# Output tiles of 16 tokens in two buffers, in place of 8 tokens in four

## The chip, the cores and the metric

The kernel runs on one core of a Trainium2 chip. The metric is the device time of a run in microseconds (us). Three runs of the kernel before gave a median of 240.93 us (240.78 to 241.42). The profile was taken of one further run of 240.54 us; its span, from the first to the last instruction of the program, is 238.8 us, and all times below that are positions in the trace count from the start of this span.

## The reference

```
batch, seq, hidden, n_experts = 16, 1024, 512, 8
k = 2
x:              (16, 1024, 512)  float32
expert_weights: (16, 1024, 2)    float32

x_expanded = x[:, :, np.newaxis, :].repeat(k, axis=2)
weights = expert_weights[..., np.newaxis]
return (x_expanded * weights).astype(np.float32)
```

Each of the 16,384 tokens is a row of 512 numbers. The output has two copies of each row, the first multiplied by the token's first weight and the second by its second weight. The expert indices are an input that is not used. 33.5 MB come in and 67.1 MB go out, and there is one multiplication for each number that goes out.

## The kernel before

The tokens are dealt to the 128 partitions in blocks: partition p holds tokens 128p to 128p + 127, so each partition has 128 tokens, which lie one after another in memory (`xr`, `outr` and `wr`, lines 27 to 33). A stretch of several tokens of one partition is therefore one contiguous row on both sides of a transfer.

All weights are loaded once, in one transfer of 128 KB issued by SyncE (line 45). The outer loop (line 47) runs over 8 input tiles of `TX` = 16 tokens for each partition. An input tile is 128 partitions x 8192 numbers, 4 MB, with rows of 32 KB, and is loaded on ScalarE's queue (line 49). The pool `x_pool` has two buffers, so a third load can be issued only when VectorE has read all of the first tile.

The inner loop (line 52) makes two output tiles of `TO` = 8 tokens from each input tile. For each token and each of its two weights, VectorE multiplies 512 numbers of the input tile by a weight, one weight for each partition, and writes them to the output tile (line 59). That is 16 multiplies for an output tile and 256 in all. Then SyncE issues the store of the output tile (line 67): 4 MB, with rows of 8 x 1024 numbers, 32 KB. The pool `o_pool` has four buffers, so the fifth output tile can be begun only when the first store has landed.

The framework puts in the waits: a multiply waits for its input tile's load and for the store that last used its output buffer; a store waits for the last multiply of its tile; a load waits for the last multiply that reads its buffer. Each engine keeps the order in which the program names its work. The order of the work is therefore set by the two queues and by the number of buffers, and by nothing else.

Of the kernel before, what the change touches and what calls it, by code (L numbers as in the profile page):

```python
# [1 line left out]

# [4 lines left out]


@with_exitstack
def kernel(  # L10
    ctx: ExitStack,
    tc: tile.TileContext,
    x: bass.AP,
    expert_indices: bass.AP,
    expert_weights: bass.AP,
    out: bass.AP,
):
    nc = tc.nc

    batch, seq, hidden = x.shape  # L20
    k = expert_weights.shape[-1]
    P = nc.NUM_PARTITIONS
    ntok = batch * seq
    assert ntok % P == 0
    A_TOTAL = ntok // P

    xr = x.rearrange("b s h -> (b s) h").rearrange("(p a) h -> p (a h)", a=A_TOTAL)
    outr = out.rearrange("b s k h -> (b s) (k h)").rearrange(
        "(p a) n -> p (a n)", a=A_TOTAL
    )  # L30
    wr = expert_weights.rearrange("b s k -> (b s) k").rearrange(
        "(p a) k -> p (a k)", a=A_TOTAL
    )
    f32 = mybir.dt.float32
    row = k * hidden

    TX = 16
    TO = 8

    w_pool = ctx.enter_context(tc.tile_pool(name="w_pool", bufs=1))  # L40
    x_pool = ctx.enter_context(tc.tile_pool(name="x_pool", bufs=2))
    o_pool = ctx.enter_context(tc.tile_pool(name="o_pool", bufs=4))

    w_tile = w_pool.tile([P, A_TOTAL * k], f32)
    nc.sync.dma_start(out=w_tile, in_=wr)

    for i in range(A_TOTAL // TX):
        x_tile = x_pool.tile([P, TX * hidden], f32)
        nc.scalar.dma_start(
            out=x_tile, in_=xr[:, i * TX * hidden : (i + 1) * TX * hidden]  # L50
        )
        for j in range(TX // TO):
            o_tile = o_pool.tile([P, TO * row], f32)
            for t in range(TO):
                at = (j * TO + t) * hidden
                for kk in range(k):
                    c = (i * TX + j * TO + t) * k + kk
                    o = t * row + kk * hidden
                    nc.vector.tensor_scalar(  # L59
                        out=o_tile[:, o : o + hidden],  # L60
                        in0=x_tile[:, at : at + hidden],
                        scalar1=w_tile[:, c : c + 1],
                        scalar2=None,
                        op0=mybir.AluOpType.mult,
                    )
            first = (i * TX + j * TO) * row
            nc.sync.dma_start(out=outr[:, first : first + TO * row], in_=o_tile)


# [1 line left out]
_INS = ['x', 'expert_indices', 'expert_weights']  # L71
_OUTS = [((16, 1024, 2, 512), 'float32')]


# [23 lines left out]
```

## Time and profile before

| what | value |
|---|---|
| time, median of 3 | 240.93 us |
| span of the profiled run | 238.8 us |
| VectorE busy | 102.5 us in 256 multiplies |
| read from and written to memory | 33.69 MB and 67.11 MB, 422 GB/s over the span |
| stores | 16 of 4096 KB, median 44.9 us from issue to landing |
| loads of the input | 8 of 4096 KB, median 23.9 us from issue to landing |
| load of the weights | 128 KB, 10.1 us from issue to landing |

On the page of the profile, the span is cut into 40 equal slices of about 6 us. Each digit of the row for DMA is the busy share of the core's 16 DMA engines in that slice in tenths, and the row of GB/s is what they moved. The queue that the page calls q1 is SyncE's (the stores and the weights), and q10 is ScalarE's (the loads of the input); for each queue the page gives the packets, the MB and the share of 16 engines' span that the packets took. In the list of waits, the three numbers are the total in us, how often, and the longest. In a list in order of time, a line has its start and length in us, the engine and line, the instruction with what it writes and reads, how many of them were joined, and in brackets the idle time before the first with what ended it. The name L59 is line 59 of the kernel.

### The profile page before, as it was taken

How to read it: one execution, taken by the hardware profiler on the slowest of the kernel's cores; microseconds unless marked ns; L12 is line 12 of the kernel's file. 1: busy time of each engine (PE TensorE's matmuls, PEld its weight loads, DVE VectorE, ACT ScalarE, POOL GpSimd, SP SyncE). 2: the span in 40 equal slices, each digit the busy share in tenths (PEclk: the TensorE clock that was granted, in tenths of full speed). 3: DMA queues.
4: the chain of work that ended last, by engine and by line, in shares of the span. 5: the costliest groups of instructions: out<-in, count | busy, mean ns of one | idle time of the engine just before them, and what ended most of it. 6: DMA issues, size and time to landing. Idle time of an engine off the chain costs nothing.

```text
span 238.8 us, 358 instructions
## 1 busy us (share of the span) xinstructions
DVE 102.5 (43%) x256; POOL 0.2 (0%) x4
## 2 busy tenths in 40 slices
DVE  0079994059701904682054910739008486400000
POOL 0000000000000000000000000000000000000000
DMA  7999999999999999999999999999999999999994
GB/s 277 447 439 417 434 380 417 439 439 439 423 423 428 439 423 412 439 439 439 439 439 434 434 439 439 412 435 428 428 423 434 434 439 439 439 439 434 434 439 214
DMA packets 3602, 100.81 MB, mean 422 GB/s; under 512 B 400, under 2 KB 528, under 8 KB 528
## 3 DMA queue, kind: packets, MB, share of 16 engines
q1 hardware_dynamic: 2448, 67.24, 65.4%
q10 hardware_dynamic: 1152, 33.55, 33.2%
q14 instruction: 2, 0.02, 0.0%
HBM read 33.69 MB, written 67.11 MB: 422 GB/s over the span
## 4 chain that ended last, share of the span: by engine, by line
DMA 62%; DVE 18%; another core or an unknown queue 5%; DVEq 0%; issue 0%
DMA out_dram<-o_tile 57%; DVE o_tile L59 18%; DMA x_tile<-in_x_dram 5%; DVEq L93 0%; DVEq L59 0%
## 5 line engine op out<-in xcount | busy, mean ns | idle before, releaser
L59 DVE TENSOR_SCALAR o_tile<-x_tile,w_tile 128x512 f32<-128x512 f32 x256 | 102.5, 480 | 103.3 <-DMA out_dram<-o_tile 74.1
L82 POOL MEMSET const-bfloat16-1.0<- 128x1 bf16 x1 | 0.1, 101 | 0.0
L82 POOL MEMSET const-uint8-127<- 128x1 uint8 x1 | 0.1, 101 | 0.0
L82 POOL MEMSET const-float32-0.0<- 128x1 f32 x1 | 0.1, 98 | 0.2 <-issue 0.2
L82 POOL MEMSET const-float32-1.0<- 128x1 f32 x1 | 0.1, 98 | 0.0
## 6 DMA issues: line engine op xcount, KB each, us to landing
out_dram<-o_tile SPq DMA_DIRECT2D x16, 4096.0 KB, 44.9
x_tile<-in_x_dram ACTq DMA_DIRECT2D x8, 4096.0 KB, 23.9
w_tile<-in_expert_weights_dram SPq DMA_DIRECT2D x1, 128.0 KB, 10.1
```

The costliest lines, as they stand in the source:

```text
L59: nc.vector.tensor_scalar(out=o_tile[:, o : o + hidden], in0=x_tile[:, at : at + hidden], scalar1=w_tile[:, c : c + 1], scalar2=None, op0= ...
L82: nc = _bacc.Bacc("TRN2", target_bir_lowering=False, num_devices=1)
```

## The change

Output tiles hold 16 tokens, as many as an input tile, so that each input tile gives one output tile of 8 MB, and a store has rows of 64 KB in place of 32 KB. There are two such output buffers in place of four of half the size, so the memory for them is the same: 128 KB of each partition. It is meant to store in fewer and longer pieces.

The code around it is written in a more general form: a list of groups, each with its tiles, each tile with the pieces in which it is loaded. Here there is one group of eight tiles with one piece each, so that `rows(x, 0, 128)` is the same split of the tokens as before, the weights are loaded in one transfer, and each input tile is loaded in one transfer of 16 tokens on ScalarE's queue, as before. A store is issued when a piece or an output tile ends, which is once for each input tile.

```diff
-    TO = 8
+    TO = 16
+    groups = [[[16], [16], [16], [16], [16], [16], [16], [16]]]
...
-    o_pool = ctx.enter_context(tc.tile_pool(name="o_pool", bufs=4))
+    o_pool = ctx.enter_context(tc.tile_pool(name="o_pool", bufs=2))
...
+    def rows(of_all, done, T):
+        return of_all[done * P : (done + T) * P, :].rearrange(
+            "(p a) n -> p (a n)", a=T
         )
...
+        for pieces in group:
+            x_tile = x_pool.tile([P, TX * hidden], f32)
+            at = 0
+            for n in pieces:
+                nc.scalar.dma_start(
+                    out=x_tile[:, at * hidden : (at + n) * hidden],
+                    in_=xr[:, (a0 + at) * hidden : (a0 + at + n) * hidden],
+                )
+                at += n
...
+            for t in range(at):
+                if t % TO == 0:
+                    o_tile = o_pool.tile([P, TO * row], f32)
                 for kk in range(k):
-                    c = (i * TX + j * TO + t) * k + kk
-                    o = t * row + kk * hidden
+                    c = (done + a0 + t) * k + kk
+                    o = t % TO * row + kk * hidden
                     nc.vector.tensor_scalar(
...
-            nc.sync.dma_start(out=outr[:, first : first + TO * row], in_=o_tile)
+                if t + 1 in ends or (t + 1) % TO == 0:
+                    nc.sync.dma_start(
+                        out=outr[:, (a0 + first) * row : (a0 + t + 1) * row],
+                        in_=o_tile[:, first % TO * row : (t % TO + 1) * row],
+                    )
+                    first = t + 1
```

More of the change, by code (lines that the diff above doesn't have):

```diff
@@ L25 @@
     A_TOTAL = ntok // P
[L27 to L33, printed above, removed]
     f32 = mybir.dt.float32
@@ L37 @@
     TX = 16
-    TO = 8
+    TO = 16
+    groups = [[[16], [16], [16], [16], [16], [16], [16], [16]]]
+    assert sum(sum(sum(t) for t in g) for g in groups) == A_TOTAL
+    xf = x.rearrange("b s h -> (b s) h")
+    of = out.rearrange("b s k h -> (b s) (k h)")
+    wf = expert_weights.rearrange("b s k -> (b s) k")
     w_pool = ctx.enter_context(tc.tile_pool(name="w_pool", bufs=1))
     x_pool = ctx.enter_context(tc.tile_pool(name="x_pool", bufs=2))
-    o_pool = ctx.enter_context(tc.tile_pool(name="o_pool", bufs=4))
+    o_pool = ctx.enter_context(tc.tile_pool(name="o_pool", bufs=2))
@@ L44 @@
     w_tile = w_pool.tile([P, A_TOTAL * k], f32)
[L45 to L50, printed above, removed]
-        )
[L52 to L55, printed above, removed]
+    def rows(of_all, done, T):
+        return of_all[done * P : (done + T) * P, :].rearrange(
+            "(p a) n -> p (a n)", a=T
+        )
@@ new lines @@
+    done = 0
+    for group in groups:
+        T = sum(sum(t) for t in group)
+        nc.sync.dma_start(
+            out=w_tile[:, done * k : (done + T) * k], in_=rows(wf, done, T)
+        )
+        done += T
+    done = 0
+    for group in groups:
+        T = sum(sum(t) for t in group)
+        xr = rows(xf, done, T)
+        outr = rows(of, done, T)
+        a0 = 0
+        for pieces in group:
[7 more added lines that the diff above has]
+                at += n
+            ends = [sum(pieces[: i + 1]) for i in range(len(pieces))]
+            first = 0
+            for t in range(at):
+                if t % TO == 0:
+                    o_tile = o_pool.tile([P, TO * row], f32)
@@ L56 @@
                 for kk in range(k):
-                    c = (i * TX + j * TO + t) * k + kk
-                    o = t * row + kk * hidden
+                    c = (done + a0 + t) * k + kk
+                    o = t % TO * row + kk * hidden
                     nc.vector.tensor_scalar(
                         out=o_tile[:, o : o + hidden],
-                        in0=x_tile[:, at : at + hidden],
+                        in0=x_tile[:, t * hidden : (t + 1) * hidden],
                         scalar1=w_tile[:, c : c + 1],
@@ L65 @@
                     )
-            first = (i * TX + j * TO) * row
-            nc.sync.dma_start(out=outr[:, first : first + TO * row], in_=o_tile)
+                if t + 1 in ends or (t + 1) % TO == 0:
+                    nc.sync.dma_start(
+                        out=outr[:, (a0 + first) * row : (a0 + t + 1) * row],
+                        in_=o_tile[:, first % TO * row : (t % TO + 1) * row],
+                    )
+                    first = t + 1
+            a0 += at
+        done += T
 _INS = ['x', 'expert_indices', 'expert_weights']
```

## The prediction

> **What bounds the kernel now.** I read the page's slices and queues first, then the waits, then the bandwidth of stretches of time, then VectorE in order of time. The page says how full the transfers are:
>
> ```profile
> span 238.8 us, 358 instructions
> ...
> DVE 102.5 (43%) x256; POOL 0.2 (0%) x4
> ...
> DMA  7999999999999999999999999999999999999994
> GB/s 277 447 439 417 434 380 417 439 439 439 423 423 428 439 423 412 439 439 439 439 439 434 434 439 439 412 435 428 428 423 434 434 439 439 439 439 434 434 439 214
> ...
> q1 hardware_dynamic: 2448, 67.24, 65.4%
> q10 hardware_dynamic: 1152, 33.55, 33.2%
> ```
>
> The reader is to see that only the first and the last of 40 slices have room. The two queues' shares add to 98.6% of the span, so about 1.4%, some 3.4 us, is all the idle time the transfers have. VectorE works 43% of the time. The waits look heavy:
>
> ```profile
> DVE o_tile L59 <- DMA out_dram<-o_tile: 74.1, 10, 12.9
> DVE o_tile L59 <- DMA x_tile<-in_x_dram: 25.3, 2, 13.3
> ```
>
> VectorE waits 74.1 us for stores to land, but while it waits the transfers run, so these waits end nothing. The kernel is bound by bytes: 100.81 MB at whatever rate the transfers hold. The question for any edit is only whether it changes that rate or lets the transfers run dry. The rate by stretch (the columns are the stretch, its length, busy VectorE and GpSimd with their counts, clock, DMA share, GB/s):
>
> ```profile
> 0.00:2.00 2.00, 0.00 (x0) 0.20 (x4) 1.00 0.09 11
> 2.00:20.00 18.00, 6.69 (x17) 0.00 (x0) 1.00 1.03 438
> 20.00:22.00 2.00, 2.00 (x6) 0.00 (x0) 1.00 0.90 311
> 22.00:24.00 2.00, 2.00 (x6) 0.00 (x0) 1.00 1.07 459
> 24.00:26.00 2.00, 2.00 (x7) 0.00 (x0) 1.00 1.06 459
> ...
> 30.00:40.00 10.00, 8.74 (x23) 0.00 (x0) 1.00 0.99 394
> 40.00:230.00 190.00, 77.08 (x192) 0.00 (x0) 1.00 1.00 433
> ```
>
> 433 GB/s is the steady rate over 190 us. Nothing moves in the first 2.0 us: the first load is issued at 0.7, so an idle set of DMA engines takes 1.3 us from issue to data. And at 22 to 26, with VectorE 9 us into its first tile, the rate is full. VectorE in order of time (start, length, work, idle before):
>
> ```profile
> 13.31 25.42 DVE L59 TENSOR_SCALAR o_tile<-x_tile,w_tile 128x512 f32<-128x512 f32 x64 [13.31 <-DMA x_tile<-in_x_dram]
> 50.73 6.42 DVE L59 TENSOR_SCALAR o_tile<-x_tile,w_tile 128x512 f32<-128x512 f32 x16 [12.00 <-DMA x_tile<-in_x_dram]
> 57.63 6.42 DVE L59 TENSOR_SCALAR o_tile<-x_tile,w_tile 128x512 f32<-128x512 f32 x16 [0.47 <-DMA out_dram<-o_tile]
> ```
>
> It starts at 13.31, when the first load has landed. 64 multiplies take 25.42 us, so one follows another every 0.40 us; 16 make a store of today, 32 use up an input tile.
>
> **What the Trainium skill says.** "DMA: Bandwidth & Descriptors", section "Where 436 GB/s comes from", puts the ceiling of the DMA engines at 435.2 GB/s. The trace holds 433, so no shape of row can win more than 0.5% of the bytes' time. Same page, "Queues, rings and completion order": each DMA engine serves the queues that have work in turn, a whole packet from each. The trace agrees that they share: the first load lands 12.6 us after its issue with no store beside it, the one issued at 26.1 takes 24.5, and it lands before the store issued at 32.4 (44.4 us to landing), so neither queue starves the other. Same page, "Anatomy of one DMA": a DMA engine never waits on a semaphore, the issuing engine waits before it hands the transfer over. The trace agrees: the third load goes out at 26.1, just when VectorE's 32nd multiply ends (13.3 + 32 x 0.40), and not before. So what is not yet issued can't fill a hole.
>
> **The change part by part.** Layout, input tiles and multiplies stay. `groups` holds one group, so `rows` cuts all 128 tokens of a partition as the old rearranges did, and the weights still load in one piece. 256 multiplies x 0.40 us = 102.5 us as before, nothing on the path. The output tile grows from 8 to 16 tokens and the buffers fall from four to two; memory is the same. Stores go from 16 of 4 MB to 8 of 8 MB.
>
> (a) Issues saved: 8 stores fewer at 0.33 us each on SyncE, 2.7 us. At nothing: SyncE only issues, under 433 GB/s of other transfers.
>
> (b) Longer rows. Before, a load has (1152 - 128)/8 = 128 packets for 4 MB beside 16 small ones, so a packet is a row of 32 KB. After, a store row is 64 KB. If it goes as one packet, half of the per-packet cost of the stores goes. Bound: nothing (it is cut in two), or all the way to the ceiling: 67.1 MB / 433 = 155.0 us against 67.1 / 435.2 = 154.2, so 0.8 us. I take 0.4.
>
> (c) The first store goes out later. Before: 13.3 + 16 x 0.40 = 19.7, and the trace has it at 19.8, while the second load is still running, so stores take over with no hole at 22 to 26. After: 32 multiplies must end, 26.1. Until then only the weights and two loads have been issued: both input buffers are full and the third load waits for the first to be read, also 26.1. Bytes in flight: 2 x 4.19 + 0.13 = 8.52 MB at 433 GB/s = 19.7 us, from 2.0 to 21.7. In the trace the second load landed at 23.9 (issued 1.1, 22.8 us) with store rows mixed in from 22, so I bound the end of its data by 21.7 and 22.7 and take 22.2. Both queues then restart from idle: 26.1 + 1.3 = 27.4. The hole is 4.7 to 5.7, I take 5.2 us. It lies wholly on the path, since later the transfers have no spare time to regain it.
>
> (d) Two buffers of twice the size. A multiply of tile i waits until store i-2 has landed and load i is there; behind it in VectorE's queue stand all later multiplies, and through them the next store and the load after next. Does this let the transfers run dry again? While VectorE makes tile i (12.8 us), store i-1 is queued whole: 8.39 MB / 433 = 19.4 us even with no load beside it. From the landing, 12.8 + 0.4 (landing to first multiply) + 1.3 (issue to data) = 14.5 us, or 17 if a load's landing is held up by one store row of 64 KB (64 KB at 433/16 GB/s = 2.4 us). Both are under 19.4, so the wait is hidden by store i-1. At nothing.
>
> (e) The joining of queues: before, 30 to 40 us shows 394 where 433 would do, 10 x (1 - 394/433) = 0.9 us lost when the first load joins a running store. After, both start together at 27.4; this may vanish or double with longer rows. I take no difference, and +-0.9 for the range.
>
> (f) The end: the last store before is issued at 205.8 and lands 32.2 us later, behind others. After, store 7 follows store 6 (19.4 us) in 12.8 us of VectorE work. The queue never empties, and both end on the same bytes. At nothing.
>
> Sum: 240.93 + 5.2 - 0.4 = 245.7 us.
>
> **The rivals.** First, loads starve: if store packets of 64 KB push the loads back until the store queue is empty, loads come in pairs. Stores 0 and 1 would run 27.4 to 66.2, load 2 to 75.9, load 3 to 85.6, while VectorE makes tile 2 from 76.3 to 89.1 and the next data start at 90.4: a hole of 4.8 us for each of three pairs of later loads. 245.7 + 3 x 4.8 = 260. For it: in turn by packet, a load would have a third of the rate rather than half. Against: a third is just what the bytes need (33.5 in, 67.1 out), so with it load i and store i-2 end together about 57, then every 29 us. Second, the other side: the hole is not there or is paid for, because long rows raise the rate. To end at 240.9 or below, they would have to save 5.2 us of 155, a store rate of 448 GB/s; no long stretch of the trace exceeds 438, and the ceiling is 435. The hole itself could only be filled by a third input buffer. It would give 240.5. Third, 64 KB rows move worse than two of 32: each per cent costs 1.55 us, so 2% gives 245.7 + 0.4 + 3.1 = 249. The trace before has only 32 KB rows and can't exclude it.
>
> **How the numbers follow.** Forecast (one hole at the start) 0.87; no slower 0.06, split between 0.03 faster and 0.03 the same; starving loads 0.04; worse rows 0.03. All but the second are slower: 0.94. The range is the forecast with its bounds, the low end 240.93 + 4.7 - 0.8 - 0.9 = 243.9, the high end 240.93 + 5.7 + 0.9 = 247.5; it leaves out the 0.13 of the rivals.
>
> **What would show it.** Between about 22.5 and 27 GB/s falls to near zero, so the fourth and fifth slices show some 6 and 5 tenths and every later one 9. VectorE runs 64 multiplies without a break from 13.3, then begins tile 2 near 57, then about every 29 us; its wait for stores and loads grows although nothing is lost there. Loads beside stores take 31 us and then some 45 to landing where the median was 23.9. q1 falls from 2448 packets to 8 x 144 + 144 = 1296 if a row is one packet, to 2320 if it is cut in two, and then loads keep half the rate and land sooner. A second hole near 86 us would speak for starving loads; a steady rate under 430 for worse rows. The prediction is wrong if the slices stay full from 18 to 30 us, or if the steady rate passes 440.

## The result, and the profile after

The changed kernel took 250.48 us (247.97 to 250.78, six runs) against 241.15 us: 1.035 times the kernel before, 95% interval 1.0297 to 1.0404. Run again on another chip it gave 1.0243 (1.0199 to 1.0286), where the kernel before had 243.19 us. Since chips differ by as much as 2 us, ratios are compared below, each with the kernel before on the same chip. The comparison leaves out single times more than 1.5% above the lowest of the same version, which are four of the six of loads16 (249.9 to 260.9 us) and two of the six of tail32 (244.9 to 249.6 us), so the ratios of these two are lower bounds.

The page of the changed kernel is from a run of 248.15 us, one of the two faster of the six; the other four lie between 250.4 and 250.8 us and have no trace, so what follows accounts for the smaller loss:

```profile
span 246.4 us, 337 instructions
...
DMA  7995798999899999999989989999998999999892
GB/s 274 433 452 223 234 427 367 436 447 431 378 442 468 410 399 473 415 394 442 463 383 426 511 383 410 469 426 394 458 479 367 431 495 399 458 394 489 372 489 128
...
q1 hardware_dynamic: 1296, 67.24, 63.6%
q10 hardware_dynamic: 1152, 33.55, 32.4%
```

The fourth and fifth slices are half empty, as forecast; q1 has the forecast 1296 packets, so a 64 KB row is one packet. But there are digits of 8 up to the end, where the page before had none. The rate by stretch (stretch, its length in us, VectorE, GpSimd, clock, DMA share, GB/s):

```profile
20.00:22.00 2.00, 2.00 (x6) 0.00 (x0) 1.00 0.72 311
22.00:24.00 2.00, 2.00 (x6) 0.00 (x0) 1.00 0.00 0
24.00:26.00 2.00, 2.00 (x6) 0.00 (x0) 1.00 0.00 0
26.00:28.00 2.00, 2.00 (x6) 0.00 (x0) 1.00 1.38 524
28.00:30.00 2.00, 2.00 (x6) 0.00 (x0) 1.00 0.34 66
30.00:40.00 10.00, 8.91 (x23) 0.00 (x0) 1.00 1.00 401
40.00:200.00 160.00, 63.79 (x160) 0.00 (x0) 1.00 1.00 430
200.00:240.00 40.00, 12.76 (x32) 0.00 (x0) 1.00 1.01 437
240.00:242.00 2.00, 0.00 (x0) 0.00 (x0) 1.00 0.38 164
242.00:244.00 2.00, 0.00 (x0) 0.00 (x0) 1.00 0.60 262
```

The lines of the kernel before that belong beside these and are not shown above:

```profile
26.00:28.00 2.00, 2.00 (x7) 0.00 (x0) 1.00 0.84 360
28.00:30.00 2.00, 2.00 (x7) 0.00 (x0) 1.00 1.15 492
...
234.00:236.00 2.00, 0.00 (x0) 0.00 (x0) 1.00 0.72 311
236.00:238.00 2.00, 0.00 (x0) 0.00 (x0) 1.00 0.16 66
```

Three things are to be seen. Nothing moves from 22 to 26. After the restart there is a second dent, 66 GB/s at 28 to 30 (in stretches as short as these the figures jump, so 26 to 30 should be read together: 295 GB/s). And the end is ragged: from 240 us to the end of the span, 6.4 us moved what takes 2.0 at the full rate; before, the 4.8 us from 234 (311 and 66 GB/s, then nothing) moved what takes 1.7. That is 1.3 us more lost. Against 433 GB/s, the stretch from 20 to 40 us lost 6.6 us; the same stretch before lost 1.3 (311, 459, 459, 360, 492, 394). That is 5.3 of the 7.6 us between the two profiled spans. 430 for 433 over 160 us is 1.1, and with the 1.3 of the end the sum is 7.7.

VectorE in order of time, and its waits:

```profile
13.47 25.43 DVE L83 TENSOR_SCALAR o_tile<-x_tile,w_tile 128x512 f32<-128x512 f32 x64 [13.47 <-DMA x_tile<-in_x_dram]
61.48 12.76 DVE L83 TENSOR_SCALAR o_tile<-x_tile,w_tile 128x512 f32<-128x512 f32 x32 [22.58 <-DMA x_tile<-in_x_dram]
90.48 12.76 DVE L83 TENSOR_SCALAR o_tile<-x_tile,w_tile 128x512 f32<-128x512 f32 x32 [16.24 <-DMA x_tile<-in_x_dram]
```

```profile
DVE o_tile L83 <- DMA x_tile<-in_x_dram: 118.0, 7, 22.6
```

The 64 multiplies without a break, the period of 29 us and the loads' 45 us to landing (median 45.4) came as forecast; the third tile began at 61.5 where the forecast had 57. The load is now the last to land, and its 45.4 us are longer than the 29 us after which the next load is issued, so that a load is always under way. Before, the median was 23.9 us, and for part of the time no load was under way.

### The profile page after: what moved, and what is told of

It is laid out like the page before. It is cut to its first block, busy times and chain, and to the rows that moved or that the text cites. A ratio compares the mean times of both kernels' runs of the same rounds, so it can differ in the third digit from the quotient of the medians.

```text
span 246.4 us, 337 instructions
## 1 busy us (share of the span) xinstructions
DVE 102.0 (41%) x256; POOL 0.2 (0%) x4
## 3 DMA queue, kind: packets, MB, share of 16 engines
q1 hardware_dynamic: 1296, 67.24, 63.6%
## 4 chain that ended last, share of the span: by engine, by line
DMA 56%; DVE 26%; another core or an unknown queue 7%; DVEq 0%; issue 0%
DMA x_tile<-in_x_dram 56%; DVE o_tile L83 26%; DVEq L123 0%; DVEq L83 0%
## 6 DMA issues: line engine op xcount, KB each, us to landing
x_tile<-in_x_dram ACTq DMA_DIRECT2D x8, 4096.0 KB, 45.4
w_tile<-in_expert_weights_dram SPq DMA_DIRECT2D x1, 128.0 KB, 10.3
```

## The experiments

Theory 1 was that the whole loss comes from the late first store: the hole and the slow restart. Its rival, theory 2, that rows of 64 KB cost by themselves.

**The changed kernel again.** 

> The changed kernel once more, to see how far its time spreads. The runs so far lie near 248 and near 250.5, the profiled one at 248.15. If the second figure is a property of the kernel, it shows up here too; if it is one of a chip, all runs here lie within 1 us of each other.

1.0243 (1.0199 to 1.0286), median 248.51 us. The spread stays: single runs reach 250.49 here too.

**early8: no hole, long rows.**

```diff
-                if t + 1 in ends or (t + 1) % TO == 0:
+                if t + 1 in ends or (t + 1) % TO == 0 or (a0 == 0 and t + 1 == 8):
```

> The first output tile is stored in two halves, the first after 16 multiplies; all other stores keep their rows of 64 KB and there are still two buffers. Theory 1 (all of the loss comes from the first store's lateness: an empty stretch of 4.9 us from 22.2 to 27.1 and a slow restart after it): the loss goes, 240.0 to 241.5 us, no slice under 9 tenths after the first. Theory 2 (the hole gives 4.9 us and the rest of the loss belongs to rows of 64 KB wherever they are): 243 us or more.

1.0158 (1.011 to 1.0207), 246.63 us, and no empty stretch at 22 to 26, but a trickle at the end:

```profile
22.00:26.00 4.00, 4.00 (x12) 0.00 (x0) 1.00 1.10 475
...
238.00:240.00 2.00, 0.00 (x0) 0.00 (x0) 1.00 0.15 66
240.00:242.00 2.00, 0.00 (x0) 0.00 (x0) 1.00 0.15 66
```

Theory 1 falls: of the 5.3 us that the changed kernel lost on this chip, 3.4 are still there without the hole.

**halves_late: every tile stored in two halves, both written after the tile's multiplies.**

```diff
-                    nc.sync.dma_start(
-                        out=outr[:, (a0 + first) * row : (a0 + t + 1) * row], ...)
+                    for half in range(0, t + 1 - first, 8):
+                        lo = first + half
+                        nc.sync.dma_start(
+                            out=outr[:, (a0 + lo) * row : (a0 + lo + 8) * row], ...)
```

> Every tile is stored in two halves with rows of 32 KB, but both are issued only after all 32 multiplies, so the first store is as late as in the changed kernel. Theory 1: the hole and the slow restart stay, 247 to 250 us. Theory 2: the hole alone stays, 245 to 246 us, and the stretch from 28 to 36 us is as full as later ones.

0.9964 (0.9945 to 0.9982). The edit missed its aim: a store waits only for the multiplies that write its own half, so the first half went out after 16 of them and there was no hole. What it shows instead is that two large buffers with rows of 32 KB cost nothing.

**held: the kernel before, the first store written after the second tile.**

```diff
+            if i == 0 and j == 0:
+                held = o_tile
+                continue
+            if i == 0 and j == 1:
+                nc.sync.dma_start(out=outr[:, 0 : TO * row], in_=held)
```

> The kernel before (8 tokens, four buffers, rows of 32 KB) with one edit: the first store is held back until the second tile is done, and then both are issued. Theory 1: it gets the hole and the slow restart, 246.5 to 249 us. Theory 2: the hole alone, 245 to 246 us. If two large buffers instead of four small ones were the cause, it would stay near 241.

1.0005 (0.9984 to 1.0025): for the same reason it sent its first store as early as before, at 20.3 us, and serves only as a control.

**hole_small: the kernel before with a real hole.** The last multiply of the first output tile is moved behind those of the second.

```diff
+        order = [(t, kk) for t in range(TX) for kk in range(k)]
+        if i == 0:
+            order.remove((7, 1))
+            order.insert(30, (7, 1))
...
```

> The kernel before (8 tokens, four buffers, rows of 32 KB), with the order of the first input tile's multiplies changed so that its first output tile is ready only at multiply 31 of 32, and so really stored late (held, as written, still sent its store at 19.8). Theory A (the hole costs its whole length, about 4.9 us, plus 2 for the restart, whatever the rows are): 5 to 7 us above the kernel before on the same chip. Theory B (rows of 64 KB are the larger part of the loss, and a hole is partly won back because it lines the 16 engines up again): 1.5 to 3 us above.

1.0192 (1.0158 to 1.0226), 246.99 against 242.35 us: 4.6 us, between the figures of its two theories. The first store went out at 25.9 us. Its stretches:

```profile
20.00:22.00 2.00, 2.00 (x6) 0.00 (x0) 1.00 0.72 311
22.00:24.00 2.00, 2.00 (x6) 0.00 (x0) 1.00 0.00 0
24.00:26.00 2.00, 2.00 (x6) 0.00 (x0) 1.00 0.00 0
26.00:28.00 2.00, 2.00 (x6) 0.00 (x0) 1.00 0.90 377
28.00:30.00 2.00, 2.00 (x6) 0.00 (x0) 1.00 1.11 410
30.00:40.00 10.00, 8.91 (x23) 0.00 (x0) 1.00 0.93 351
```

The same empty stretch, with four buffers and rows of 32 KB. From 26 to 40 it ran at 363 GB/s, the changed kernel at 371, so the slow restart too belongs to the hole and not to the long rows.

**hole_halves: the same hole with two large buffers and rows of 32 KB** (the same reordering, and the stores of halves_late). 

> Output tiles of 16 tokens in two buffers, stored as two halves with rows of 32 KB; the first tile's first half is ready only at multiply 31, all later halves go out as soon as they are made. It is the hole with the large buffers and short rows. Theory A: 5 to 7 us above the kernel before. Theory B: 1 to 3 us above, and thus 2 to 4 us below the changed kernel.

1.0145 (1.0116 to 1.0174), 246.14 us: 3.8 us, again between the two. So with rows of 32 KB the hole is worth 3.8 to 4.6 us, whichever buffers there are. That is less than it loses on the spot: from 20 to 40 us, hole_halves lost 5.1 us more than rows32_late below, on the same chip, but its span is only 3.7 us longer (244.1 for 240.4). The rest came back later.

**rows32_late: early8 with each late store cut into two of 32 KB rows.** Second half first, so that both wait for all multiplies.

```diff
+                    for lo in (0, 8) if a0 == 0 else (8, 0):
...
```

> As early8 in everything but the length of the rows: the first tile is stored in two halves as each is made, every later tile only when all its 32 multiplies are done, but as two stores with rows of 32 KB (second half first). If the 64 KB rows are what costs early8 its 3.4 us over the kernel before: within 1 us of halves_late, 0.99 to 1.00 of the kernel before. If it is the lateness of whole-tile stores with two buffers: as early8, about 1.015.

0.9983 (0.9957 to 1.0008). The lateness of whole-tile stores costs nothing; what early8 pays for goes with the 64 KB rows.

**quarters: rows of 16 KB.** A store whenever (t + 1) % 4 == 0. 

> Output tiles of 16 tokens in two buffers, stored in quarters of 4 tokens with rows of 16 KB as they are made; the first store goes out after 8 multiplies. If a longer row makes the engines drift apart (64 KB against 32 KB), a shorter one should hold them closer: the last engines end within 1.5 us of the first, and the time is equal to halves_late or up to 1 us below. If 32 KB is the best of both, since each row has a fixed cost: 0.5 to 1.5 us above halves_late.

1.0014 (0.9991 to 1.0037), and 0.8 us above rows32_late on the same chip. Store rows shorter than the loads' rows cost little or nothing.

**early8_again, tail32, head32: where the long rows cost.** In tail32 only the middle four tiles, in head32 only the last three have rows of 64 KB. The loop over the stores of a tile, first in tail32, then in head32:

```diff
+                    for lo, n in [(0, 8), (8, 8)] if a0 == 0 else [(0, 16)] if a0 < 80 else [(8, 8), (0, 8)]:
...
```

```diff
+                    for lo, n in [(0, 8), (8, 8)] if a0 == 0 else [(8, 8), (0, 8)] if a0 < 80 else [(0, 16)]:
...
```

> The kernel early8 once more, as the measure for the three beside it: first store in two halves, no hole, all later stores with rows of 64 KB. It gave 1.016 of the kernel before; the same within 0.5% is expected under every theory.

> As early8, but the last three tiles are stored as two stores with rows of 32 KB each, late as before; the four tiles in the middle keep rows of 64 KB. Theory tail (rows of 64 KB cost because engines that are one row behind end one long row later, and since the last stores run with no loads beside them to even it out): the loss goes, 0.998 to 1.004 of the kernel before. Theory mixing (the loss grows wherever rows of 64 KB alternate with the loads' rows of 32 KB): most of it stays, 1.008 to 1.014.

> The mirror of it: rows of 32 KB for the first five tiles, of 64 KB for the last three, two of which run after the last load. Theory tail: the loss of early8 stays, 1.010 to 1.016 of the kernel before. Theory mixing: it goes for the most part, 0.998 to 1.005.

early8_again 1.0228 (1.0181 to 1.0276), tail32 1.0154 (1.0099 to 1.0209), head32 0.9992 (0.9974 to 1.001). early8_again lost more than early8, by more than the expected 0.5%, and tail32 a little more than expected. Long rows in the middle, beside loads, cost; long rows at the end do not. The loss itself shows in two places. These are the steady stretch and the end of early8_again:

```profile
40.00:200.00 160.00, 63.78 (x160) 0.00 (x0) 1.00 1.01 422
...
238.00:240.00 2.00, 0.00 (x0) 0.00 (x0) 1.00 1.21 524
240.00:242.00 2.00, 0.00 (x0) 0.00 (x0) 1.00 0.38 164
242.00:244.00 2.00, 0.00 (x0) 0.00 (x0) 1.00 0.08 33
244.00:246.00 2.00, 0.00 (x0) 0.00 (x0) 1.00 0.08 33
```

In the steady stretch head32 held 431 GB/s on the same chip, so that early8_again lost 3.3 of the 6.9 us between the two spans (248.1 and 241.2) there, with a DMA share of 1.01, that is, with its engines busy. The rest was lost at the end. There, 33 GB/s is little more than one engine of 16 at its full rate (433 / 16 = 27), and a share of 0.08 is 1.3 engines of 16: for 4 us the kernel waits for one engine or so. The Trainium skill, "DMA: Bandwidth & Descriptors", section "The descriptor swizzle", says that each partition's row goes to a fixed engine. The trace has no engine numbers, but the trickle fits: an engine that has fallen behind keeps its rows, and no other can take them.

**loads16: loads in two pieces with rows of 16 KB, stores in halves of 32 KB.**

```diff
-    groups = [[[16], [16], [16], [16], [16], [16], [16], [16]]]
+    groups = [[[8, 8]] * 8]
```

> The input tiles are loaded in two pieces with rows of 16 KB, and stored in halves with rows of 32 KB as they are made: store rows are twice as long as load rows, as in the changed kernel, but half as long in themselves; there is no hole, since the first store goes out after half a load. If it is the unlike length of the rows of the two queues that costs: 1.008 or more of the kernel before. If it is the 64 KB: 0.995 to 1.003.

1.0289 (1.0241 to 1.0338), as bad as the changed kernel, with no row over 32 KB and no hole. Its steady rate is 423 GB/s, and its end has the same trickle:

```profile
240.00:242.00 2.00, 0.00 (x0) 0.00 (x0) 1.00 0.34 147
242.00:244.00 2.00, 0.00 (x0) 0.00 (x0) 1.00 0.08 33
244.00:246.00 2.00, 0.00 (x0) 0.00 (x0) 1.00 0.08 33
```

**equal16: the loads of loads16, stores in quarters.** 

> Loads in two pieces with rows of 16 KB, as in loads16, but stores in quarters with rows of 16 KB too, so that the rows of both queues are alike again. If store rows twice as long as load rows are what costs, wherever they are met: 0.995 to 1.005 of the kernel before, and engines that end within 2.5 us of each other. If it is the loads of 16 KB rows, or their number, that made loads16 slow: 1.02 or more, as there.

0.995 (0.9931 to 0.9968), and the end is sharp:

```profile
200.00:236.00 36.00, 12.59 (x32) 0.00 (x0) 1.00 1.01 432
236.00:238.00 2.00, 0.00 (x0) 0.00 (x0) 1.00 0.46 197
238.00:240.00 2.00, 0.00 (x0) 0.00 (x0) 1.00 0.00 0
```

So neither 64 KB nor short loads are at fault in themselves: with two queues, store rows twice as long as the load rows beside them cost, rows alike do not. The next pair asked whether the turns that a DMA engine takes between the two queues, row by row, are the cause.

**one_queue and one_queue32: loads behind stores on SyncE's queue, no turns.**

```diff
-                nc.scalar.dma_start(
+                nc.sync.dma_start(
...
+        ahead = [load(0), load(1)]
...
+            if i + 2 < len(group):
+                ahead.append(load(i + 2))
```

> As early8 (first store in two halves, then rows of 64 KB), but the loads go out on SyncE's queue too, each behind the store of the tile before last, so that loads and stores follow one another and never take turns row by row. If the loss of early8 comes of the turns between rows of 64 KB and 32 KB: 0.992 to 1.003 of the kernel before. If rows of 64 KB cost by themselves: 1.012 or more.

> One queue as well, with rows of 32 KB (stores in halves as they are made) and the first input tile loaded in two pieces. It says what the turns cost when both rows have 32 KB: 0.992 of the kernel before, as first_piece, if they cost nothing; 0.985 to 0.990 if they do.

1.0175 (1.0132 to 1.0219) and 1.0135 (1.0104 to 1.0167). one_queue came out as if long rows cost by themselves, but one_queue32 fits neither of its figures: without any turns, and with rows of 32 KB, there is a loss. So one queue has a loss of its own, and one_queue can't tell what its long rows cost. Beside one_queue32, which has the early first piece besides, they cost 0.4%, within the intervals, where with two queues they cost 1.6 to 2.3%. The pair therefore doesn't rule the turns out as the cause of the loss in early8; it shows that a kernel can lose without them. The end of one_queue32:

```profile
236.00:238.00 2.00, 0.00 (x0) 0.00 (x0) 1.00 0.83 360
238.00:240.00 2.00, 0.00 (x0) 0.00 (x0) 1.00 0.38 164
240.00:242.00 2.00, 0.00 (x0) 0.00 (x0) 1.00 0.11 49
```

Ragged again, and its rate from 40 to 200 us is 426 GB/s. What the costly versions seem to share is seen in the time of a load to landing (tile and queue, count, size, median us), here of tail32, of head32 and of one_queue32, whose first tile makes the line of two loads:

```profile
x_tile<-in_x_dram ACTq DMA_DIRECT2D x8, 4096.0 KB, 34.4
```

```profile
x_tile<-in_x_dram ACTq DMA_DIRECT2D x8, 4096.0 KB, 24.6
```

```profile
x_tile<-in_x_dram SPq DMA_DIRECT2D x7, 4096.0 KB, 45.5
x_tile<-in_x_dram SPq DMA_DIRECT2D x2, 2048.0 KB, 10.0
```

In every version with two queues that lost without a hole, and in the changed kernel, loads take a median of 34 to 45 us to landing, longer than the 29 us or so between the issues of two input tiles, so that one is mostly under way; in every version that lost nothing, they take 19.8 to 24.9 us, and the stores run alone for part of the time. That is a correlation over 12 versions, not a mechanism. With one queue the 45 us mean something else: they count the wait behind the stores that stand ahead of the load in its queue.

**first_piece, halves_again, first_piece_again: a version that beats both.** Large buffers, stores in halves with rows of 32 KB, and only the first input tile loaded in two pieces:

```diff
+    groups = [[[8, 8]] + [[16]] * 7]
...
+                if t + 1 in ends or (t + 1) % 8 == 0:
```

> Two large buffers, stores in halves with rows of 32 KB as they are made; only the first input tile is loaded in two pieces with rows of 16 KB, so that VectorE begins at about 8.5 us and the first store goes out near 15. All theories: nothing is gained, since the transfers are full anyway, 0.994 to 1.002 of the kernel before; a gain of over 0.6% would say that the early stores take something away.

> Output tiles of 16 tokens in two buffers, each half stored as it is made with rows of 32 KB: the same instructions as halves_late, whose stores turned out to go out early. 0.994 to 0.999 of the kernel before, if its small gain was real.

> The fastest version so far once more: 0.990 to 0.995 of the kernel before if its gain is real; with it the question whether it beats both kernels is settled.

first_piece 0.9924 (0.99 to 0.9949) and again 0.9944 (0.9921 to 0.9967); halves_again 0.9983 (0.9958 to 1.0008). The early start gains about 0.5%, which I had called nothing:

```profile
20.00:30.00 10.00, 2.32 (x7) 0.00 (x0) 1.00 0.98 419
30.00:40.00 10.00, 10.00 (x26) 0.00 (x0) 1.00 1.04 443
...
236.00:238.00 2.00, 0.00 (x0) 0.00 (x0) 1.00 0.12 49
```

halves_again had 426 and 368 GB/s in the first two of these stretches and 262 in the last. From 2 to 20 us first_piece is the slower one (410 GB/s, against 426 to 12 us and 446 from there), so it wins back more than it gives away. The stores that join early seem to do so with less loss; that reason was only argued.

## Why the prediction was wrong

- **Bound and (c), the hole: right in place and size.** The transfers were the bound, and the hole came where it was put: nothing moved from 22 to 26, and the next transfers were issued at 26.3. Predicted 5.2 us; the stretch from 20 to 40 us lost 5.3 more than before. About 1.0 of that is the joining, which (e) had at nothing, so that the two figures agree so closely is partly luck. That nothing would regain the hole was wrong: as a whole it cost 4.6 (hole_small) and 3.8 (hole_halves).
- **(b), longer rows: wrong, and the step that failed.** It took 64 KB rows for a small gain, 0.4 us, from half of a packet's fixed cost. early8, which has the long rows and no hole, lost 1.6% and 2.3%, 3.4 and 5.7 us between the medians. I had bounded this term from below by nothing and from above by the ceiling of 435.2 GB/s, as if it could only gain (and the trace before holds 438 from 2 to 20 us, over that ceiling). What the runs show in its place is that the row's length beside that of the loads matters: stores of 64 KB rows beside loads of 32 KB (early8) and of 32 KB beside 16 KB (loads16) lost, rows alike (rows32_late, equal16), shorter ones (quarters) and long ones at the end (head32) did not. How the length brings the loss about is open. The third rival had the sign, and its 2% even the size (249 us), but was given 0.03; its mark, a steady rate under 430, did not show in the changed kernel (430); early8_again had 422.
- **(d), two buffers: right.** halves_late and rows32_late, 0.996 and 0.998, show that with rows of 32 KB neither fewer buffers nor later stores cost.
- **(e), the joining: too small by 1.0 us.** It allowed for a double loss and took no difference; from 26 to 40 us the changed kernel lost 2.0 us against 433 GB/s, the kernel before 1.0.
- **(f), the end at nothing: wrong.** It took the 16 engines as one. As the rate of the last microseconds tells, they end apart, which cost the changed kernel 1.3 us more than the kernel before, and early8_again a trickle of 4 us.
- **The first rival: rightly small.** No second hole appears; loads lagged without starving. But I took the lockstep of loads and stores, "with it load i and store i-2 end together", as a sign of health and forecast its 45 us to landing as harmless; with two queues such long landings mark every costly version without a hole.

Sum: 3.8 to 4.6 for the hole and 3.4 to 5.7 for the long rows would make 7.2 to 10.3 us; the two sets of runs gave 9.3 and 5.3 (248.51 against 243.19). The forecast lacked the second term, but the terms do not simply add. On the chip of the second set, the profiled run of the changed kernel lost 5.4 us more than that of early8 from 20 to 40 us (311 GB/s for 2 us, 135 for 8 and 417 for 10, against 344, 446 and 394), and yet its span is only 1.8 us longer (246.4 for 244.6): after the hole, it lost 3.6 us less. Why is not shown.

**What stays open.** How long store rows beside shorter load rows cost time is not settled: neither why the engines move less while busy (early8_again) nor why they end apart. The turns between unlike rows may be the cause; one_queue32 shows only that there is a loss without them as well. Every load of the input and every store here has 128 rows, so longer rows are also larger transfers, and no run separates the two. A version with rows of 64 KB in which loads pause was not tried, except at the end (head32), nor were load rows of 64 KB.

## What to carry to other kernels

When the transfers are full from end to end, an edit is priced by where they run dry, by the rate that they hold, and by how evenly the 16 engines end, not by its count of transfers. Before making tiles larger, find the moment at which the first store can go out and compare it with the end of the data already in flight. And treat the row lengths of two queues that run side by side as a setting to be tried, not as the longer the better: here, store rows no longer than the load rows were safe. Read the steady rate, and the last few microseconds of it, where an engine that has fallen behind shows as a trickle.

## What was not expected of the hardware

The Trainium skill, "DMA: Bandwidth & Descriptors", section "Issuing engines are not separate DMA queues", says that issuing from several engines only saves the time of the sequencer. Here the queue mattered more: one_queue32 and first_piece have the same rows and the same tiles, and differ in one queue for two, and with it in that a load stands behind the stores issued before it; 1.0135 against 0.9924 and 0.9944, about 2%. Restarting two queues on an empty set of DMA engines was slower than joining one to the other: in the changed kernel 26 to 40 us ran at 371 GB/s (295 and 401), and in hole_small at 363, where the kernel before, with a load that joins running stores, had 403.
